# The query and key columns of four head pairs in the second layer, taken as seven half products in place of eight, with two gates between them and the values later

## The chip, the core and the metric

One core of a Trainium2 chip runs the whole kernel. The metric is the device time of one execution in microseconds (us). TensorE (PE in the profile, PEld for its weight loads) multiplies; VectorE (DVE), ScalarE (ACT) and GpSimd (POOL) do the elementwise work; the queue of SyncE (SP) issues most transfers, and GpSimd's own queue issues those that add to what lies in the destination. Each engine takes its instructions in the order in which the program has them, and waits on semaphores of the others.

## What is computed

The input x has 512 tokens of 1024 numbers, all float32. Two layers follow each other, and each is: norm, one wide input projection, a mixer over the tokens, a gate, an output projection, and a sum with x. The change touches only the second layer:

```python
def mixer_b(hn, w_in, w_out, q_gain, k_gain, rpb):      # hn = rms_norm(x, g)
    proj = hn @ w_in                                    # 512 x 1024 @ 1024 x 4096
    q, k, v, gate = jnp.split(proj, 4, axis=-1)
    q = rms_norm(q.reshape(b, s, N_HEADS, HEAD_DIM), q_gain) * (HEAD_DIM ** -0.5)
    k = rms_norm(k.reshape(b, s, N_HEADS, HEAD_DIM), k_gain)
    ...                                                 # attention on an 8 x 64 grid, 16 heads
    y = y * jax.nn.silu(gate)
    return y @ w_out
```

There are 16 heads of 64 columns. The kernel works on pairs of heads, hc = 0 to 7, of 128 columns each.

## The kernel before

**Products.** A float32 matrix is held as two rounded parts, high and low (`hn_h`, `hn_l` for the normed x; `wh`, `wl` for weights), and a product is three matmuls of 128x512 (`mm3`, line 353): high by high, high by low, low by high. One weight tile of 128x512 is loaded as half of a raw tile `wraw` (128x1024, eight of them), rounded by ScalarE (`cast`, line 173), and its low part is a subtraction `wl<-wraw,wh` on VectorE or GpSimd (`rest`, line 180). `Plan` (line 195) lists these jobs in the order of their use and says when a raw tile is loaded.

**Order of the work.** The order on TensorE is the program's order. A generator `main` walks through the projections and yields after every three matmuls or so; a generator `side` has the attention, and `run` lets it go on whenever a clock that counts the modelled matmul time has passed what `side` asked for (`later_on`, line 367, is a timer on that clock; `yield "wait", key, delay` waits for a stamp). For the other engines a scheduler decides the order at build time. What it decided can be listed from the built program.

**Second layer, main stream.** `B_MAIN` (line 43) gives the blocks in order: `("qk", n)` is queries and keys of pairs 2n and 2n+1, 512 columns (`main_qk`, line 1318), `("v", n)` values of four pairs (`main_v`), `("g", n)` the gate of one pair (`main_g`, line 1354). A block `qk` or `v` is 96 matmuls, a gate 24. `hn_h` and `hn_l` hold x times the norm's gain but not divided by the norm of the token: the division comes when results leave the accumulators, by `rs_n` (one number for each token) as ScalarE's scale, and for the gates by `rs_half`, a row of it for all partitions that `spread` makes by four transposes on TensorE (`pa<-ident,rs_n`).

**Second layer, side stream.** `side_b(hc)` (line 1379) scales a pair's queries and keys by the norms of its heads (`rawk<-rawk,rs`, VectorE, 128x1024), transposes them on TensorE (`tp<-ident,rawk`, four for the queries, four for the keys), rounds and splits them (`qh`, `ql`, `kh`, `kl`), makes scores (24 matmuls `log<-kh,qh` and the like), then exponents and their transposes. `weigh_b(hc)` multiplies with the values. `unit` (line 140) is a chain of nine small VectorE instructions (`nv`, `rs`, `na`) that makes the head norms from sums of squares (`ss<-sq`).

**First layer.** It already takes seven half products of the Strassen-Winograd form for its pairs 1 to 7 (`Plan.mixed`, line 232, and `main_a`). For that, x is first multiplied by its norm in place (`scale_x`, line 551: eight VectorE instructions `pt<-pt,pa`), split again (`renorm`, line 560), and four sums of its quarters are made and split (`mix`, line 564: `mixed<-...`, `mix_h`, `mix_l`). Weight sums are made in the raw tiles, by transfers that add (`Plan.add`, GpSimd's queue) and by VectorE (`Plan.sum`, `wraw<-wraw`).

Of the kernel before, what the change touches and what calls it, by code (L numbers as in the profile page):

```python
# [42 lines left out]
B_MAIN = [("qk", 0), ("v", 0), ("g", 0), ("qk", 1), ("g", 1), ("g", 2), ("qk", 2),  # L43
          ("g", 3), ("qk", 3), ("v", 1), ("g", 4), ("g", 5), ("g", 6), ("g", 7)]
B_COLS = {"qk": 512, "v": 512, "g": P}
# [5 lines left out]
def tile_hybrid_encoder(  # L51
# [143 lines left out]
    class Plan:  # L195
# [36 lines left out]
        def mixed(self, hc):  # L232
            b, j = hc * A_HC, len(self.jobs)
            b11, b21, b12, b22 = ([self.raw(b + 2048 * n + 1024 * i) for i in range(2)] for n in range(4))
            gate = self.raw(b - A_HC + 1152 * KT)
            v = self.raw(b - A_HC + 1024 * KT)
            t2 = [self.raw(None) for _ in range(2)]
            late = hc == 1
# [27 lines left out]
    for hc in range(1, NHC):  # L266
        plan.mixed(hc)
# [12 lines left out]
    for kind, _ in B_MAIN:  # L280
        plan.plain(at_b, B_COLS[kind], KT)
        at_b += B_COLS[kind] * KT
    outs(B_OUT)

    def lead(raw):
        return 4 if raw.first < start_jobs else 12 if raw.first < mixed_jobs else 6
# [685 lines left out]
    class turner:  # L972
# [12 lines left out]
        def send(self, dst, wait, pace, key):  # L985
# [8 lines left out]
            def read(b):  # L994
                src = d[b].rearrange("(a k) x -> k a x", a=4)
# [322 lines left out]
    def main_qk(n):  # L1318
# [24 lines left out]
    def main_v(n):  # L1343

        if not n:
            st["v"] = wk.tile([P, 4, 512], F32, tag="rawq", name="rawv", bufs=1)

        def evac(i, acc):
            act.activation(st["v"][:, i, :], acc, AF.Copy, scale=rs_n[:, i : i + 1])

        yield from project(tile_of(hn_h), tile_of(hn_l), 512, evac, ("yb", 3, "y") if n else None)
        stamp["v", n] = clock[0]

    def main_g(hc):
        acc = []
        yield from project_t(acc)
# [4 lines left out]
        src = acc[0]  # L1361
        if hc == 3:
            act.copy(gt, src)
            src = gt
        tc.keep_in_program_order(vec.tensor_mul(gt, src, st["rs_half"]))
# [131 lines left out]
    def main():  # L1497
# [7 lines left out]
        for kind, n in B_MAIN:  # L1505
            yield from {"qk": main_qk, "v": main_v, "g": main_g}[kind](n)
        yield from out_product("yb", sink_b)

    def side():
# [11 lines left out]
        for _ in scale_x():  # L1521
# [68 lines left out]
def _layout(x, norm_gain, a_w_in, a_w_out, a_q_gain, a_k_gain, t5_bias,  # L1590
# [23 lines left out]
    for kind, n in B_MAIN:  # L1614
        parts.append(cols(wb, [D * i + P * hc for i, hc in {
            "qk": [(0, 2 * n), (1, 2 * n), (0, 2 * n + 1), (1, 2 * n + 1)],
            "v": [(2, 4 * n + j) for j in range(4)],
            "g": [(3, n)],
        }[kind]]))
# [35 lines left out]
```

## Time and profile before

| | |
|---|---|
| median of 3 runs | 823.32 us (822.88 to 825.62) |
| the profiled execution | 823.05 us, of which its span (first to last instruction) is 821.3 us |
| granted TensorE clock, mean | 0.998 |
| busy share: PE, DVE, ACT, POOL | 99%, 74%, 64%, 29% |
| second layer's `spread` to the end of the span | 578.06 to 821.3 us |

The page gives busy time by engine, the chain of work that ended last, and groups of equal instructions. The trace behind it answers by stretch of time: a row of the timeline is start, length, engine, line and what was written from what, with the idle time before it and what ended that idle time in square brackets. Matmuls overlap, so the length of one is not what one costs. Most instructions of a helper share one line (L347 for matmuls, L87 for nearly all of the other engines), so rows are told apart by their tiles.

### The profile page before, as it was taken

Reading aid. Unit: us, or ns where it says so; the run is one execution under the profiler, and the core shown is the slowest. Engines: PE = TensorE matmul, PEld = TensorE weight load, DVE = VectorE, ACT = ScalarE, POOL = GpSimd, SP = SyncE. Lnnn points to the kernel's source line nnn. Section 1 sums busy time; section 2 is a strip of 40 time slices with the busy share of each in tenths; the row PEclk is TensorE's granted clock in tenths of the full one; section 3 lists DMA queues with packets and bytes.
Section 4 is the critical chain, followed back from the end, with each engine's and each line's share of the span. In section 5 each row is a group of like instructions: output and inputs, shape, how many; then the busy total and the mean of one; then the engine's idle time right before and its main releaser. Section 6 shows DMA issues by size and latency. Waiting matters only on the chain.

```text
span 821.3 us, 17411 instructions
## 1 busy us (share of the span) xinstructions
PE 812.4 (99%) x6410; PEld 659.0 (80%) x6410; DVE 610.3 (74%) x1546; ACT 522.3 (64%) x1075; POOL 235.5 (29%) x194
## 2 busy tenths in 40 slices
PE   9999999999999999999999999999999999999998
PEld 7877878788888888888888888788888887788776
DVE  7898996897887787787887886657546769776553
ACT  8668766846856856856856848554567476766340
POOL 0041402442532622622622616312111122112120
PEclk9999999999999999999999999999999999999999
DMA  9327666576585785785785664283254564634132
GB/s 348 148 65 174 169 173 161 107 213 186 125 221 165 161 212 142 162 209 146 164 206 146 143 213 157 76 314 137 102 169 144 138 198 139 197 115 139 36 103 103
DMA packets 54869, 131.92 MB, mean 161 GB/s; under 512 B 6784, under 2 KB 24384, under 8 KB 54656
## 3 DMA queue, kind: packets, MB, share of 16 engines
q1 hardware_dynamic: 48304, 108.27, 41.8%
q0 software_dynamic: 6048, 22.02, 14.7%
q8 instruction: 50, 0.82, 0.4%
q10 hardware_dynamic: 432, 0.52, 0.2%
q14 instruction: 35, 0.29, 0.1%
HBM read 111.73 MB, written 11.72 MB: 150 GB/s over the span
## 4 chain that ended last, share of the span: by engine, by line
PE 91%; DVE 4%; ACT 3%; issue 1%; DMA 0%; DVEq 0%; SPq 0%; ACTq 0%
PE acc L347 76%; PE o L347 6%; PE log L347 5%; PE tp L351 4%; DVE wl L87 1%; ACT p L87 1%; ACT wh L87 1%; DVE mixed L87 1%; ACT rawk L87 1%; DMA wraw<-in_w 0%; DVE pt L87 0%; DVE p L87 0%; DVE rawq L87 0%; PE pk L347 0%; DVE rawk L87 0%
## 5 line engine op out<-in xcount | busy, mean ns | idle before, releaser
L87 ACT CAST wh<-wraw 128x512 fp32r<-128x512 f32 (+1 forms) x344 | 206.7, 611 | 133.2 <-PE acc L347 104.9
L87 POOL TENSOR_TENSOR wl<-wraw,wh 128x512 fp32r<-128x512 f32 (+1 forms) x126 | 170.7, 1369 | 409.5 <-PE acc L347 172.5
L87 DVE TENSOR_TENSOR wl<-wraw,wh 128x512 fp32r<-128x512 f32 (+1 forms) x218 | 166.3, 766 | 60.5 <-PE acc L347 36.4
L347 PE MATMUL acc<-wh,hn_h 128*128 128x512 f32 x424 | 171.6, 406 | 0.6 <-ACT wh L87 0.3
L347 PE MATMUL acc<-wl,hn_h 128*128 128x512 f32 x424 | 165.3, 391 | 0.4 <-DVE wl L87 0.3
L347 PE MATMUL acc<-wh,hn_l 128*128 128x512 f32 x424 | 165.3, 391 | 0.0
L87 ACT ACTIVATE p<-p,mn 128x256 f32<-128x256 f32 (+2 forms) x248 | 137.9, 583 | 35.1 <-DVE mn L87 35.0
L347 PEld LDWEIGHTS acc<-wh,hn_h 128*128 128x128 f32 x424 | 79.5, 188 | 20.0 <-ACT wh L87 2.1
L347 PEld LDWEIGHTS acc<-wh,hn_l 128*128 128x128 f32 x424 | 79.6, 188 | 17.3
L347 PEld LDWEIGHTS acc<-wl,hn_h 128*128 128x128 f32 x424 | 79.8, 188 | 16.3 <-DVE wl L87 1.7
L347 PE MATMUL acc<-wh,mix_h 128*128 128x512 f32 x224 | 89.6, 400 | 0.0
L347 PE MATMUL acc<-wl,mix_h 128*128 128x512 f32 x224 | 88.1, 393 | 0.3 <-DVE wl L87 0.2
L347 PE MATMUL acc<-wh,mix_l 128*128 128x512 f32 x224 | 87.8, 392 | 0.0
L347 PE MATMUL acc<-hn_h,wh 128*128 128x512 f32 x192 | 78.4, 409 | 0.0
L347 PE MATMUL acc<-hn_h,wl 128*128 128x512 f32 x192 | 75.1, 391 | 0.0
L347 PE MATMUL acc<-hn_l,wh 128*128 128x512 f32 x192 | 75.0, 391 | 0.0
L87 DVE TENSOR_REDUCE ss<-sq 128x8 f32<-128x512 f32 (+1 forms) x80 | 44.0, 573 | 27.5 <-ACT sq L87 26.9
L87 POOL DMA_DIRECT2D wraw<-in_w x42 | 38.7, 935 | 82.4 <-DVE wl L87 35.7
L87 DVE STREAM_TRANSPOSE pt<-p 128x512 f32<-128x512 f32 (+1 forms) x60 | 40.9, 688 | 15.0 <-ACT p L87 14.2
L347 PE MATMUL acc<-y_h,wh 128*128 128x512 f32 x128 | 51.7, 404 | 0.0
L347 PEld LDWEIGHTS acc<-wh,mix_h 128*128 128x128 f32 x224 | 42.4, 189 | 10.2 <-issue 1.8
L347 PEld LDWEIGHTS acc<-wl,mix_h 128*128 128x128 f32 x224 | 42.4, 189 | 9.8 <-DVE wl L87 0.8
(152 smaller groups left out, 1330.8 us busy)
## 6 DMA issues: line engine op xcount, KB each, us to landing
wraw<-in_w SPq DMA_DIRECT2D x119, 512.0 KB
wraw<-in_w POOLq DMA_DIRECT2D x42, 512.0 KB, 7.3
pt<-pt SPq DMA_DIRECT2D x106, 64.0 KB
td<-tr SPq DMA_DIRECT2D x24, 224.0 KB
pt<-td SPq DMA_DIRECT2D x24, 224.0 KB
e<-l_d SPq DMA_DIRECT2D x32, 112.0 KB
wraw<-in_w SPq DMA_DIRECT2D x6, 384.0 KB
e<-l_d SPq DMA_DIRECT2D x16, 128.0 KB
```

The lines of the kernel that those rows point to most:

```text
L87: m = f(*args, **kw)
L347: nc.tensor.matmul(o, l, r, **kw)
L351: nc.tensor.transpose(o, i, ident)
```

## The change

Blocks 1 and 2 of the queries and keys (pairs 2 to 5) become one block `("u", 1)`. In it the 512 tokens and the 1024 rows of the product are halved, and seven products of half size in tokens and rows replace eight: 7 x 24 = 168 matmuls in place of 2 x 96 = 192. Gates 1 and 2 stand between the first products. The order of blocks becomes qk 0, gate 0, u (with gates 1 and 2), values 0, qk 3, gates 3 and 4, values 1, gates 5 to 7; before, values 0 came second.

To that end, after `spread`, x is multiplied by its norm in place (`scale_x`, now called for both layers), each slice of `hn_h` and `hn_l` is made anew as soon as gate 0 has used the old one (`renorm`, on ScalarE and in turn VectorE and GpSimd), and `mix_b` makes four sums of quarters on VectorE, their rounded parts on ScalarE and the low parts on GpSimd, into the space of `y_h` and `y_l`. Later blocks leave the accumulators by a copy, since x is already divided; gates 1 to 7 are halved by ScalarE. The weights of u are planned as those of the first layer's pairs, with four transfers that add into weights, two that add into weight sums, and two sums on VectorE. The side stream's delays change, and weighing of pairs 0 and 1 moves behind values 0.

```diff
-B_MAIN = [("qk", 0), ("v", 0), ("g", 0), ("qk", 1), ("g", 1), ("g", 2), ("qk", 2),
-          ("g", 3), ("qk", 3), ("v", 1), ("g", 4), ("g", 5), ("g", 6), ("g", 7)]
+B_MAIN = [("qk", 0), ("g", 0), ("u", 1), ("v", 0), ("qk", 3), ("g", 3), ("g", 4), ("v", 1),
+          ("g", 5), ("g", 6), ("g", 7)]
...
+        if kind == "u":
+            first_u = len(plan.jobs)
+            plan.mixed(at_b, at_b + 1024 * KT, at_b + 1152 * KT)
+            jobs_u = range(first_u, len(plan.jobs))
...
-    def project_t(acc):
+    def project_t(acc, after=None):
...
             mm3(acc[0], h, l, hn_h[:, k, :], hn_l[:, k, :], k == 0, k == KT - 1)
             yield
+            if after:
+                yield "xb", k
+                after(k)
...
-    def scale_x():
-
-        pa = spread()
+    def scale_x(pa, layer, key):
+
         for k in range(KT):
             xk = x_all[:, k, :]
-            vec.scalar_tensor_tensor(xk, xk, ng[:, 0, k : k + 1], pa, op0=ALU.mult, op1=ALU.mult)
-            stamp["xn", k] = 0
+            vec.scalar_tensor_tensor(xk, xk, ng[:, layer, k : k + 1], pa, op0=ALU.mult, op1=ALU.mult)
+            stamp[key, k] = 0
             yield 0
...
+    def mix_b():
+
+        x11, x12, x21, x22 = quarters()
+        t = wk.tile([P, 2, KH, H], F32, tag="rawq", name="mixed", bufs=1)
...
+        a, b = t[:, 0], t[:, 1]
+
+        def put(n, out, op, x, y):
+            op(out, x, y)
+            act.copy(mh[:, n], out)
+            later_on(1200, partial(split, n, out))
+
+        def split(n, out):
+            pol.tensor_sub(ml[:, n], out, mh[:, n].bitcast(F32))
+            stamp["mixb", n] = 0
+
+        for i, args in enumerate((
+            (0, a, vec.tensor_sub, x21, x22), (1, b, vec.tensor_sub, a, x11),
+            (3, b, vec.tensor_add, b, x12), (2, a, vec.tensor_sub, x11, x21),
+        )):
+            later_on(2000 + 4000 * i, partial(put, *args))
...
+    def main_u(n):
...
+        yield from product(a, hn(0, 0), True, keep)
+        yield from main_g(n)
+        yield from product(a, hn(KH, 0), False, put11)
+        yield from main_g(n + 1)
+        for m, acc, first, put in ((0, c, True, put_v), (1, b, True, put_u), (3, c, False, put12), (2, b, False, put22)):
+            yield "mixb", m
+            yield from product(acc, mixed(m), first, put, None if m else ("qk", 2 * n - 1))
+        yield from product(b, hn(KH, H), False, put21)
+        normed_b(n, r1, s1)
+        normed_b(n + 1, r2, s2)
...
     def main_g(hc):
         acc = []
-        yield from project_t(acc)
+        yield from project_t(acc, None if hc else renorm)
...
-        if hc in (1, 3, 5, 6):
-            yield "wait", ("qk", hc - 1), {1: 16000, 3: 15000, 5: 15500}.get(hc, 12000)
+        if hc in (0, 2):
+            yield "wait", ("raw", hc), 4500
         else:
-            yield "wait", ("raw", hc), 5500 if hc == 2 else 4500
+            yield "wait", ("qk", hc - 1), {1: 8000, 7: 12000}.get(hc, 9500)
...
-        act.mul(st["rs_half"], spread(), 0.5)
+        pa = spread()
+        act.mul(st["rs_half"], pa, 0.5)
         stamp["rs", "all"] = 0
+        for _ in scale_x(pa, 1, "xb"):
+            pass
+        mix_b()
         for hc in range(NHC - 2):
-            if hc >= 2:
-                yield "wait", *((("qk", hc - 1), 11000) if hc % 2 else (("raw", hc), 1500))
+            if hc == 3:
+                yield from weigh_b(0)
+                yield from weigh_b(1)
+            yield from side_b(hc)
+            if hc > 3:
                 yield from weigh_b(hc - 2)
-            yield from side_b(hc)
```

**What it moves on VectorE.** The place is the start of the second layer, from the sums of squares of qk 0 to the scaling of pair 0 that the first transposes of queries wait for. `ss` are sums of squares, `nv`, `na` and `rs` the chain of `unit`, `wl` low parts of weights, `rawk<-rawk,rs` the scaling. Before:

```order
L87 TENSOR_REDUCE ss_7118<-sq_7319 128x8
L87 TENSOR_SCALAR nv_7323<-ss_7118 128x32
L87 TENSOR_SCALAR rs_7322<-nv_7323 128x32
L87 TENSOR_TENSOR na_7324<-rs_7322 128x32
L87 TENSOR_TENSOR na_7324<-na_7324,nv_7323 128x32
L87 SCALAR_TENSOR_TENSOR na_7324<-na_7324 128x32
L87 SCALAR_TENSOR_TENSOR rs_7322<-na_7324,rs_7322 128x32
L87 TENSOR_TENSOR na_7324<-rs_7322 128x32
L87 SCALAR_TENSOR_TENSOR na_7324<-na_7324,nv_7323 128x32
L87 SCALAR_TENSOR_TENSOR rs_7322<-na_7324,rs_7322 128x32
L87 TENSOR_TENSOR wl_7376<-wraw_7180,wh_7345 128x512
L87 TENSOR_TENSOR rawk_155<-rawk_155,rs_7322 128x4x256 x2
```

The chain of nine stands in one piece, one weight split follows it, and the scaling of both pairs comes next.

Now, at the same place, first the part that ends with the second sum of quarters (`pt` is x, `hn_l` the low part made anew, `mixed` the sums of quarters):

```order
L87 SCALAR_TENSOR_TENSOR pt_97<-pt_97,pa_7303 128x512 x8
L87 TENSOR_TENSOR wl_7351<-wraw_6994,wh_7275 128x512
L87 TENSOR_REDUCE ss_7124<-sq_7322 128x8
L87 TENSOR_TENSOR hn_l_93<-pt_97,hn_h_92 128x512
L87 TENSOR_REDUCE ss_7124<-sq_7332 128x8
L87 TENSOR_TENSOR hn_l_93<-pt_97,hn_h_92 128x512
L87 TENSOR_TENSOR mixed_7317<-pt_97 128x1024
L87 TENSOR_TENSOR wl_7414<-wraw_7036,wh_7376 128x512
L87 TENSOR_TENSOR hn_l_93<-pt_97,hn_h_92 128x512 x2
L87 TENSOR_SCALAR nv_7336<-ss_7124 128x32
L87 TENSOR_TENSOR wl_7426<-wraw_7036,wh_7412 128x512
L87 TENSOR_TENSOR mixed_7317<-mixed_7317,pt_97 128x1024
```

The eight instructions of `scale_x` stand ahead of two of the sums of squares, and the chain of `unit` has only begun when two sums of quarters are done. After a further weight split, the chain's `rs`, a weight sum `wraw_7596<-wraw_6964,wraw_7219` and the chain's first `na`, the rest of the stretch is:

```order
L87 TENSOR_TENSOR mixed_7317<-pt_97 128x1024
L87 TENSOR_TENSOR na_7337<-na_7337,nv_7336 128x32
L87 SCALAR_TENSOR_TENSOR na_7337<-na_7337 128x32
L87 SCALAR_TENSOR_TENSOR rs_7335<-na_7337,rs_7335 128x32
L87 TENSOR_TENSOR mixed_7317<-mixed_7317,pt_97 128x1024
L87 TENSOR_TENSOR na_7337<-rs_7335 128x32
L87 SCALAR_TENSOR_TENSOR na_7337<-na_7337,nv_7336 128x32
L87 SCALAR_TENSOR_TENSOR rs_7335<-na_7337,rs_7335 128x32
L87 TENSOR_TENSOR rawk_155<-rawk_155,rs_7335 128x4x256
L87 TENSOR_TENSOR gt_7403<-acc_7347,rs_half_7302 128x512
L87 TENSOR_TENSOR rawk_155<-rawk_155,rs_7335 128x4x256
```

All four sums of quarters stand ahead of the scaling of pair 0, and the last of them lies in the middle of the chain. On TensorE the first transposes of queries stand where they stood: 51 matmuls behind the four transposes of `spread` (9 of qk 0, then 42 of the values before; 9 of qk 0, 24 of gate 0 and 18 of u's first product now).

**What it moves on GpSimd.** At the same place GpSimd had only weight splits, `wl<-wraw,wh`. Now it has, from the last split that belongs to the first tiles of u (`DMA` are transfers that add to weights, `y_l` the low parts of the sums of quarters):

```order
L87 TENSOR_TENSOR wl_7277<-wraw_6964,wh_7271 128x512
L87 DMA wraw_6964<-in_w 128x1024
L87 TENSOR_TENSOR wl_7378<-wraw_6994,wh_7349 128x512
L87 TENSOR_TENSOR hn_l_93<-pt_97,hn_h_92 128x512 x2
L87 DMA wraw_6994<-in_w 128x1024
L87 TENSOR_TENSOR hn_l_93<-pt_97,hn_h_92 128x512 x2
L87 TENSOR_TENSOR wl_7439<-wraw_7088,wh_7424 128x512
L87 TENSOR_TENSOR y_l_6262<-mixed_7317,y_h_6261 128x1024 x2
L87 DMA wraw_7597<-in_w 128x1024
L87 TENSOR_TENSOR y_l_6262<-mixed_7317,y_h_6261 128x1024 x2
```

Four splits of x and four of the sums of quarters have come between the weight splits. VectorE's third and fourth `mixed` write over the first and second, and so wait for the first two of these `y_l`.

More of the change, by code (lines that the diff above doesn't have):

```diff
@@ L230, in add, with mixed @@
             )
-        def mixed(self, hc):
-            b, j = hc * A_HC, len(self.jobs)
+        def mixed(self, b, gate, v, late=False):
+            j = len(self.jobs)
             b11, b21, b12, b22 = ([self.raw(b + 2048 * n + 1024 * i) for i in range(2)] for n in range(4))
-            gate = self.raw(b - A_HC + 1152 * KT)
-            v = self.raw(b - A_HC + 1024 * KT)
+            gate, v = self.raw(gate), self.raw(v)
             t2 = [self.raw(None) for _ in range(2)]
-            late = hc == 1
             order = (b11, gate, b21, b11, t2, b22, b12, v, t2) if late else (b11, gate, b21, v, b11, t2, b22, b12, t2)
@@ L266, in tile_hybrid_encoder @@
     for hc in range(1, NHC):
-        plan.mixed(hc)
+        b = hc * A_HC
+        plan.mixed(b, b - A_HC + 1152 * KT, b - A_HC + 1024 * KT, hc == 1)
     plan.plain((NHC - 1) * A_HC + 1024 * KT, 128, KT)
@@ L280, in tile_hybrid_encoder @@
     for kind, _ in B_MAIN:
-        plan.plain(at_b, B_COLS[kind], KT)
+        if kind == "u":
+            first_u = len(plan.jobs)
+            plan.mixed(at_b, at_b + 1024 * KT, at_b + 1152 * KT)
+            jobs_u = range(first_u, len(plan.jobs))
+        else:
+            plan.plain(at_b, B_COLS[kind], KT)
         at_b += B_COLS[kind] * KT
@@ L285, in lead @@
     def lead(raw):
-        return 4 if raw.first < start_jobs else 12 if raw.first < mixed_jobs else 6
+        return 4 if raw.first < start_jobs else 12 if raw.first < mixed_jobs or raw.first in jobs_u else 6
     behind, begun = [], []
@@ L562, in renorm, with quarters @@
         (pol if k % 2 else vec).tensor_sub(hn_l[:, k, :], x_all[:, k, :], hn_h[:, k, :].bitcast(F32))
+    def quarters():
+        return (x_all[:, k : k + KH, t : t + H] for t in (0, H) for k in (0, KH))
+    def mix_b():
+        x11, x12, x21, x22 = quarters()
+        t = wk.tile([P, 2, KH, H], F32, tag="rawq", name="mixed", bufs=1)
+        st["mix"] = [
+            st[y].rearrange("p (n k) (j h) -> p n (k j) h", n=4, j=2) for y in ("y_h", "y_l")
+        ]
+        mh, ml = st["mix"]
+        a, b = t[:, 0], t[:, 1]
[11 more added lines that the diff above has]
+            later_on(2000 + 4000 * i, partial(put, *args))
     def mix():
-        x11, x12, x21, x22 = (x_all[:, k : k + KH, t : t + H] for t in (0, H) for k in (0, KH))
+        x11, x12, x21, x22 = quarters()
         t = wk.tile([P, 2, KH, H], F32, tag="tr", name="mixed", bufs=1)
@@ L1322, in evac @@
         def evac(i, acc):
-            act.activation(raw[:, i, :], acc, AF.Copy, scale=rs_n[:, i : i + 1])
+            if n:
+                act.copy(raw[:, i, :], acc)
+            else:
+                act.activation(raw[:, i, :], acc, AF.Copy, scale=rs_n[:, i : i + 1])
             squares(raw[:, i, :], ss, i, 8)
@@ L1327, in main_qk, with keep, put11, put_v @@
         yield from project(tile_of(hn_h), tile_of(hn_l), 512, evac, guard)
+        normed_b(n, raw, ss)
+    def main_u(n):
+        r1, r2, s1, s2, a, b, c = part(n), part(n + 1), sums(), sums(), [], [], []
+        hn = lambda k0, t0: lambda k: (t[:, k0 + k, t0 : t0 + H] for t in (hn_h, hn_l))
+        mixed = lambda m: lambda k: (t[:, m, k, :] for t in st["mix"])
+        def keep(i, acc):
+            act.copy(r1[:, 2 + i, :], acc)
+        def put11(i, acc):
+            act.copy(r1[:, i, :], acc)
+            squares(r1[:, i, :], s1, i, 8)
+        def put_v(i, acc):
+            vec.tensor_sub(r2[:, 2 + i, :], acc, r1[:, 2 + i, :])
+        def put_u(i, acc):
+            vec.scalar_tensor_tensor(r2[:, i, :], acc, -1.0, r1[:, 2 + i, :], op0=ALU.mult, op1=ALU.subtract)
+        def put12(i, acc):
+            t = r2[:, i, :]
+            vec.tensor_add(t, t, acc)
+            squares(t, s2, i, 8)
+        def put22(i, acc):
+            t = r2[:, 2 + i, :]
+            vec.tensor_sub(t, t, acc)
+            squares(t, s2, 2 + i, 8)
+        def put21(i, acc):
+            t = r1[:, 2 + i, :]
+            vec.tensor_add(t, t, acc)
+            squares(t, s1, 2 + i, 8)
+        yield from product(a, hn(0, 0), True, keep)
[8 more added lines that the diff above has]
+        normed_b(n + 1, r2, s2)
+    def normed_b(n, raw, ss):
         rs = wk.tile([P, 32], F32, tag="rs", name="rs")
@@ L1360, in main_g @@
         eg = wk.tile([P, S], F32, tag="eg", name="eg", bufs=1)
[L1361 to L1365, printed above, removed]
+        if hc:
+            act.mul(gt, acc[0], 0.5)
+        else:
+            tc.keep_in_program_order(vec.tensor_mul(gt, acc[0], st["rs_half"]))
         act.activation(eg, gt, AF.Tanh)
@@ L1505, in main @@
         for kind, n in B_MAIN:
-            yield from {"qk": main_qk, "v": main_v, "g": main_g}[kind](n)
+            yield from {"qk": main_qk, "v": main_v, "g": main_g, "u": main_u}[kind](n)
         yield from out_product("yb", sink_b)
@@ L1520, in side @@
         stamp["rs", "a"] = 0
-        for _ in scale_x():
+        for _ in scale_x(spread(), 0, "xn"):
             pass
@@ L1614, in _layout @@
     for kind, n in B_MAIN:
[L1615 to L1619, printed above, removed]
+        for kind, n in [("qk", n), ("qk", n + 1), ("g", n), ("g", n + 1)] if kind == "u" else [(kind, n)]:
+            parts.append(cols(wb, [D * i + P * hc for i, hc in {
+                "qk": [(0, 2 * n), (1, 2 * n), (0, 2 * n + 1), (1, 2 * n + 1)],
+                "v": [(2, 4 * n + j) for j in range(4)],
+                "g": [(3, n)],
+            }[kind]]))
     parts += outs(wbo)
```

5 lines of the change are left out of this document (3 added, 2 removed).

## The prediction

> **What bounds the kernel now.** I read the page first: its span, the busy shares, and the chain of work that ended last.
>
> ```profile
> span 821.3 us, 17411 instructions
> PE 812.4 (99%) x6410; PEld 659.0 (80%) x6410; DVE 610.3 (74%) x1546; ACT 522.3 (64%) x1075; POOL 235.5 (29%) x194
> PE 91%; DVE 4%; ACT 3%; issue 1%; DMA 0%; DVEq 0%; SPq 0%; ACTq 0%
> L347 PE MATMUL acc<-wh,hn_h 128*128 128x512 f32 x424 | 171.6, 406 | 0.6 <-ACT wh L87 0.3
> ```
>
> TensorE has work 99% of the time and is 91% of the chain. A busy TensorE is not proof of a full one, so next came the waits of TensorE, longest first. Beside the 1.4 us before its first matmul the two largest are:
>
> ```profile
> PE log L347 <- ACT k L87: 1.2, 2, 0.7
> PE tp L351 <- ACT rawk L87: 1.0, 1, 1.0
> ```
>
> So it waits almost nowhere, and both ways of changing the time are plain: fewer matmuls shorten it, and any new wait of TensorE lengthens it in full. The mean of 406 ns in the group's row is not the price of a matmul, since matmuls overlap. The price comes from the chain, asked for the stretch in which the second layer starts (start, length, what, how many):
>
> ```profile
> 578.06 0.44 PE pa L351 x4
> 578.49 11.59 PE acc L347 x51
> 590.09 0.44 PE tp L351 x4
> 590.52 2.78 PE acc L347 x12
> 593.30 0.44 PE tp L351 x4
> 593.74 2.09 PE acc L347 x9
> 595.83 1.63 PE log L347 x24
> ```
>
> 51 matmuls of 128x512 in 11.59 us are 0.227 us each. The rows also give the place on which the prediction turns: the first transposes of queries (`tp`) come 11.59 us after `spread`'s (`pa`), before and after the change, because 51 matmuls lie between in both orders. What they wait for is VectorE's scaling of pair 0. The timeline of VectorE there, before:
>
> ```profile
> 578.80 0.69 DVE L87 TENSOR_REDUCE ss<-sq 128x8 f32<-128x512 f32 x1 [0.64 <-ACT sq L87]
> 583.49 0.18 DVE L87 TENSOR_SCALAR nv<-ss 128x32 f32<-128x32 f32 x1
> 583.70 0.18 DVE L87 TENSOR_SCALAR rs<-nv 128x32 int32<-128x32 int32 x1
> 586.06 1.12 DVE L87 TENSOR_TENSOR wl<-wraw,wh 128x512 fp32r<-128x512 f32 x1 [0.59 <-ACT wh L87]
> 587.10 2.35 DVE L87 TENSOR_TENSOR rawk<-rawk,rs 128x1024 f32<-128x1024 f32 x2
> ...
> 578.00:596.00 18.00, 18.00 (x89) 14.69 (x89) 10.46 (x21) 8.48 (x16) 3.89 (x3) 1.00 0.26 87
> ```
>
> The two scalings run from 587.10 to 589.45, the first done at 588.3: it is 1.8 us early. The last row is from the view by stretches (length, then busy us of PE, PEld, DVE, ACT, POOL): VectorE was busy for 10.46 of 18 us, so 7.5 us were free, part of them behind the scaling.
>
> **The change part by part.**
>
> *Fewer matmuls.* 192 become 168. 24 x 0.227 = 5.45 us less, all of it on the path. Nothing else of TensorE's main stream changes in number: gates, values and output products only trade places, and the end of the order (the last pair's scores, weights and the output product) is the same.
>
> *What VectorE gets ahead of pair 0's scaling.* By the order it has eight `pt<-pt,pa`, four `hn_l`, four `mixed`, one weight sum and two more weight splits. The first layer has all of them; here VectorE's rows, back to back:
>
> ```profile
> 28.41 5.36 DVE L87 SCALAR_TENSOR_TENSOR pt<-pt,pa 128x512 f32<-128x512 f32 x8 [1.10 <-PE pa L351]
> 33.69 0.69 DVE L87 TENSOR_TENSOR wl<-wraw,wh 128x512 fp32r<-128x512 f32 x1
> 34.29 0.68 DVE L87 TENSOR_REDUCE ss<-sq 128x8 f32<-128x512 f32 x1
> ...
> 54.58 0.68 DVE L87 TENSOR_TENSOR wl<-wraw,wh 128x512 fp32r<-128x512 f32 x1
> 55.18 0.68 DVE L87 TENSOR_TENSOR hn_l<-pt,hn_h 128x512 fp32r<-128x512 f32 x1
> ...
> 62.84 1.22 DVE L87 TENSOR_TENSOR wraw<-wraw 128x1024 f32<-128x1024 f32 x1
> 63.98 0.69 DVE L87 TENSOR_TENSOR wl<-wraw,wh 128x512 fp32r<-128x512 f32 x1
> 64.58 1.22 DVE L87 TENSOR_TENSOR mixed<-mixed,pt 128x1024 f32<-128x1024 f32 x1
> ```
>
> From start to start: eight `pt` 5.28 us, a 512-wide instruction 0.60, a 1024-wide one 1.14; a small one of the chain takes 0.21 (583.49 to 583.70). So 5.28 + 4 x 0.60 + 5 x 1.14 + 2 x 0.60 = 14.6 us are added. Were all the 7.5 free us ahead of the scaling, and with the 1.8 by which it was early, 14.6 - 7.5 - 1.8 = 5.3 us would still be left. VectorE cannot be in time.
>
> *How late, at least.* Follow the order as if every engine ran undisturbed. The second sum of squares starts at 578.80, so the `pt` start at 579.4 and end at 584.7. Then five 512-wide instructions (587.7), the first `mixed` (588.8), three 512-wide, `nv` and one split (591.5), the second `mixed` (592.6). The fourth `mixed` writes over the second, whose rounded part (ScalarE) and low part (GpSimd) must be taken first. Their rows from the first layer:
>
> ```profile
> 65.83 1.05 ACT L87 CAST mix_h<-mixed 128x1024 fp32r<-128x1024 f32 x1 [0.33 <-DVE mixed L87]
> 47.05 1.38 POOL L87 TENSOR_TENSOR hn_l<-pt,hn_h 128x512 fp32r<-128x512 f32 x1 [1.78 <-ACT hn_h L87]
> 50.68 2.90 POOL L87 TENSOR_TENSOR mix_l<-mixed,mix_h 128x1024 fp32r<-128x1024 f32 x1 [2.25 <-PE acc L347]
> 51.24 3.41 DVE L87 TENSOR_TENSOR mixed<-mixed,pt 128x1024 f32<-128x1024 f32 x1
> 585.33 1.29 POOL L87 TENSOR_TENSOR wl<-wraw,wh 128x512 fp32r<-128x512 f32 x1 [4.15 <-PE acc L347]
> ```
>
> 592.6 + 1.05 + 2.90 + 1.22 = 597.8, three small ones of the chain 598.4, the scaling 1.18 (half of 2.35): 599.6. TensorE, due at 590.1, would wait 9.5 us.
>
> *How late, if the two engines exclude each other.* The row at 51.24 says that they do: VectorE's sum, 1.22 us alone, took 3.41, and it ended at 54.65, 1.07 us after GpSimd's `mix_l` (50.68 + 2.90 = 53.58). The split at 586.06 shows the same: 1.12 in place of 0.69, beside GpSimd's from 585.33. Instructions of VectorE that read only one operand, or one from an accumulator, show no such stretch (the `pt` and `ss` above are of that kind). So from 584.7 on, lengths add. GpSimd, which has just finished a split then (its buffer comes free with the first half of gate 0, 578.5 + 21 x 0.227 = 583.3, plus 1.29), must do four `hn_l`, one split and two `y_l` before the fourth `mixed`: 4 x 1.38 + 1.29 + 2 x 2.90 = 12.6 us. VectorE does four splits and four `hn_l` (4.8), five 1024-wide (5.7), nine small ones (1.9) and the scaling (1.18): 13.6 us; its two `ss` may run beside GpSimd. 584.7 + 12.6 + 13.6 = 610.9, a wait of 20.8 us. I take this end, since the rows show the exclusion each time that both want two operands from memory; 9.5 remains the lower bound.
>
> A part of this wait comes earlier, at the first product's third matmul, which needs the first new `hn_l`; it is the same delay, not a second one. Behind the waiting transposes stand all matmuls: TensorE's queue has nothing else to do.
>
> The Trainium skill (SBUF — State Buffer, section "SBUF: two separate sides") says that the port pair these two engines share belongs to whichever instruction starts first, for its whole length, and that the other blocks. Read as turns, one instruction each, that rule gives the sum of this text, 840.0; this trace has a case in which GpSimd went twice in a row (the rows at 79.36 and 79.99 below), and by that the time would be 845.8.
>
> *The clock.* After waits the trace shows a slower TensorE. The two waits of the scores in the first layer (the 1.2 us above, around 78 us) were followed by this (by stretches, the third column from the end is the granted clock; then TensorE's rows):
>
> ```profile
> 79.00:82.00 3.00, 3.00 (x72) 2.29 (x73) 2.48 (x2) 1.48 (x2) 3.00 (x4) 0.70 0.74 115
> 82.00:85.00 3.00, 3.00 (x12) 2.35 (x11) 2.96 (x8) 0.62 (x1) 2.04 (x3) 0.73 1.00 190
> ...
> 81.44 0.63 PE L347 MATMUL acc<-wl,mix_h 128*128 128x512 f32 x1
> 81.86 0.63 PE L347 MATMUL acc<-wh,mix_l 128*128 128x512 f32 x1
> ```
>
> Matmuls 0.42 apart, and (0.30 + 0.27) x 3 / 0.5 = 3.4 us at half clock. That is eight matmuls at 0.2 us more: 1.6 us, once, after the long wait.
>
> *What costs nothing.* Twelve more weight tiles are rounded and split in u, its ten combining instructions run on VectorE, and gates are halved on ScalarE. In the 52 us from 596 on, VectorE and ScalarE are free for about a third:
>
> ```profile
> 596.00:622.00 26.00, 26.00 (x138) 21.37 (x138) 13.71 (x44) 15.56 (x41) 3.89 (x3) 1.00 0.54 167
> 622.00:648.00 26.00, 26.00 (x150) 21.20 (x149) 20.38 (x55) 18.13 (x45) 6.51 (x5) 1.00 0.60 168
> ```
>
> Free on VectorE: 12.3 + 5.6 = 17.9 us. Added: twelve splits at most (7.2), ten combinations (6.0), one sum (1.1): 14.3. It fits, with little to spare; if it doesn't, the third rival is the price. The transfers that add are issued by GpSimd and are due several tiles later, as in the first layer; among the waits of TensorE none is put down to a transfer.
>
> *The sum*, against the profiled execution's own 823.05 us (its span and 1.75 us around; the median of the runs, 823.32, is 0.03% above): 823.05 - 5.45 + 20.8 + 1.6 = 840.0 us.
>
> **The rivals.**
>
> *The engines share after all.* Then the wait is 9.5 us: 823.05 - 5.45 + 9.5 + 1.6 = 828.7, and anything up to about 835 if some instructions slip past each other. For it: a few 1024-wide scalings kept their 1.2 us beside GpSimd. Against it: the 3.41 us. Chance 0.22.
>
> *Faster.* The scaling's lateness stays inside what the 24 matmuls save: 823.05 - 5.45 = 817.6 at best. It decides at a scaling done by 590.1 + 5.4 = 595.5, 4.1 us before my lower bound. For it: 7.5 us of VectorE were free. Against it: even with every free moment used, the 5.3 us left above eat up the 5.45 saved. Chance 0.07. That the seven products are not there is no rival: the order has 24 rows fewer on TensorE.
>
> *More waits behind the first.* GpSimd can hold the place twice in a row:
>
> ```profile
> 79.36 3.19 POOL L87 TENSOR_TENSOR wl<-wraw,wh 128x512 fp32r<-128x512 f32 x2
> 79.99 3.65 DVE L87 TENSOR_TENSOR mix_l<-mixed,mix_h 128x1024 fp32r<-128x1024 f32 x1 [0.52 <-ACT mix_h L87]
> ```
>
> If the last two `y_l` go ahead of the chain, 2 x 2.90 = 5.8 us come on top: 845.8; and if they hold VectorE between the scaling and `kl`, the scores wait some 2 us more: 848. Chance 0.15.
>
> **How the numbers follow.** The forecast (835 to 845) has 0.56. The range, 827 to 848, leaves out the faster case (0.07) and about 0.05 at either end of the other two. About 0.3% (2.5 us) is what a measurement of this kernel can tell from no change. Faster by more: 0.06; within: 0.04, from the edges of the first two rivals; slower: 0.90.
>
> **What would show it.** Right: among TensorE's waits a new one, `tp` for VectorE's `rawk`, of some 18 to 21 us, with one of about 2 us for `hn_l` before it; eight `pt` of 5.3 us after `pa`; `mixed` and `hn_l` of VectorE at 2 to 4 us beside GpSimd's `y_l`; a half clock for 3.4 us behind. Wrong: transposes less than 6 us after their old place, or VectorE's instructions keeping 0.69 and 1.22 us beside GpSimd's. A wait in the u block's later products, or for an adding transfer, would make the place wrong even if the time were right.

## The result, and the profile after

The changed kernel takes 847.87 us (median of 4 runs, 845.04 to 848.37), the kernel before 823.48 us on the same chip. The ratio is 1.0282, with a 95% interval of 1.0257 to 1.0307: slower by 24 us. The forecast was 840.0 us, in a range of 827 to 848, and slower with a chance of 0.90. The profiled execution took 848.37 us, of which its span is 846.6.

First the head of the page after:

```profile
span 846.6 us, 17500 instructions
PE 813.4 (96%) x6386; PEld 658.2 (78%) x6386; DVE 637.8 (75%) x1574; ACT 536.6 (63%) x1101; POOL 263.4 (31%) x213
```

TensorE has 24 matmuls less (6386 for 6410) and almost the same busy time, but a span 25.3 us longer: it waits now. Its waits, longest first (us in total, times, longest):

```profile
PE tp L355 <- DVE rawk L87: 21.7, 1, 21.7
PE acc L351 <- DVE rawk L87: 1.6, 2, 1.0
...
PE acc L351 <- DVE hn_l L87: 0.7, 1, 0.7
```

One row is nearly the whole result: the first transposes of the second layer's queries wait 21.7 us for VectorE's scaling of pair 0. The other two are new as well, and small: `hn_l` in the first product of u, and the accumulators of u's last product (`acc` for `rawk`).

The chain of waits around that place (start, length, what), to be held against the rows of before at 590.09 to 595.83:

```profile
611.30 2.27 DVE na L87
...
613.83 1.24 DVE rawk L87
...
615.11 1.11 PE tp L355 x4
616.22 5.08 PE acc L351 x12
621.31 0.43 PE tp L355 x4
621.74 2.09 PE acc L351 x9
...
663.08 0.41 DVE wl L87
663.48 0.60 DVE rawk L87
664.08 1.09 DVE wl L87
```

The twelve matmuls behind the transposes take 5.08 us in place of 2.78; and at 663 a second, small stop shows, where VectorE takes weight splits between the sums that empty u's accumulators.

What VectorE did until 613.83, from its timeline:

```profile
581.77 5.35 DVE L87 SCALAR_TENSOR_TENSOR pt<-pt,pa 128x512 f32<-128x512 f32 x8
...
591.05 5.21 DVE L87 TENSOR_TENSOR mixed<-pt 128x1024 f32<-128x1024 f32 x1
...
597.99 2.32 DVE L87 TENSOR_SCALAR nv<-ss 128x32 f32<-128x32 f32 x1
600.22 0.68 DVE L87 TENSOR_TENSOR wl<-wraw,wh 128x512 fp32r<-128x512 f32 x1
...
603.87 2.33 DVE L87 TENSOR_TENSOR na<-rs 128x32 f32<-128x32 f32 x1
...
608.93 2.34 DVE L87 TENSOR_TENSOR na<-rs 128x32 f32<-128x32 f32 x1
611.30 2.26 DVE L87 SCALAR_TENSOR_TENSOR na<-na,nv 128x32 f32<-128x32 f32 x1
```

And GpSimd's timeline over the same time:

```profile
591.13 2.82 POOL L87 TENSOR_TENSOR hn_l<-pt,hn_h 128x512 fp32r<-128x512 f32 x2
593.64 1.52 POOL L87 TENSOR_TENSOR wl<-wraw,wh 128x512 fp32r<-128x512 f32 x1
597.41 2.85 POOL L87 TENSOR_TENSOR y_l<-mixed,y_h 128x1024 fp32r<-128x1024 f32 x1 [2.25 <-ACT y_h L87]
603.19 2.96 POOL L87 TENSOR_TENSOR y_l<-mixed,y_h 128x1024 fp32r<-128x1024 f32 x1 [2.92 <-ACT y_h L87]
...
608.50 5.02 POOL L87 TENSOR_TENSOR y_l<-mixed,y_h 128x1024 fp32r<-128x1024 f32 x2 [1.53 <-ACT y_h L87]
```

Read the two together, by their ends. VectorE's first `mixed` starts at 591.05 and ends at 596.26, 1.1 us (its own length) after GpSimd's split ends at 595.16: it stood for three of GpSimd's instructions. Four instructions of the chain on 128x32 numbers, 0.18 us otherwise, take 2.26 to 2.34, each beside one `y_l`; one of the four, `nv<-ss`, reads a single tile. Where GpSimd is still (600.22), VectorE's 0.68 is the length of an undisturbed split. VectorE counts as busy for all of this time, but 4.0 us of the `mixed` and 2.1 of each of the four small ones, 12.4 of the 23 us from 591 on, are standing.

The clock, by stretches (third column from the end):

```profile
596.00:602.00 6.00, 0.00 (x0) 0.00 (x0) 6.00 (x8) 2.08 (x3) 2.85 (x1) 0.60 0.03 4
...
614.00:620.00 6.00, 4.89 (x14) 4.02 (x15) 4.12 (x7) 2.91 (x6) 1.28 (x1) 0.50 0.00 0
620.00:626.00 6.00, 6.00 (x44) 4.71 (x43) 2.58 (x9) 2.07 (x5) 0.00 (x0) 0.91 0.16 48
```

It falls during the wait and comes back at 621.1 (the last stretch: 0.91 is 4.9 of 6 us at full), 6 us after TensorE went on.

**Where 25.3 us come from**, by the distances between TensorE's matmuls, after against before:

| | us |
|---|---|
| 24 fewer matmuls | -5.45 |
| wait for the first `hn_l` | +0.8 |
| wait for pair 0's scaling | +21.8 |
| half clock behind it | +2.8 |
| two waits for accumulators in u's last product | +2.0 |
| pair 2's scores and small gaps | +1.0 |
| first product of the first layer | +2.3 |

The last row is not the change's: both kernels do the same there, and the profiled execution after was 2.2 us late by the first transposes of the first layer. Run again (a0_again, below), the kernel was only 0.3 us late when the second layer began, and its long wait was the same 21.7 us. There the half clock cost 2.4 us in place of 2.8.

### The profile page after: what moved, and what is told of

Its sections match the earlier page's. It is cut to its first block, busy times and chain, and to the rows that moved or that the text cites. A ratio compares the mean times of both kernels' runs of the same rounds, so it can differ in the third digit from the quotient of the medians.

```text
span 846.6 us, 17500 instructions
## 1 busy us (share of the span) xinstructions
PE 813.4 (96%) x6386; PEld 658.2 (78%) x6386; DVE 637.8 (75%) x1574; ACT 536.6 (63%) x1101; POOL 263.4 (31%) x213
## 5 line engine op out<-in xcount | busy, mean ns | idle before, releaser
L87 ACT CAST wh<-wraw 128x512 fp32r<-128x512 f32 (+1 forms) x356 | 214.0, 611 | 134.0 <-PE acc L351 113.0
L87 POOL TENSOR_TENSOR wl<-wraw,wh 128x512 fp32r<-128x512 f32 (+1 forms) x131 | 177.4, 1368 | 360.0 <-PE acc L351 171.9
L351 PE MATMUL acc<-wh,hn_h 128*128 128x512 f32 x384 | 157.4, 411 | 2.5 <-DVE rawk L87 1.6
L351 PE MATMUL acc<-wl,hn_h 128*128 128x512 f32 x384 | 151.0, 395 | 0.4 <-DVE wl L87 0.3
L351 PE MATMUL acc<-wh,hn_l 128*128 128x512 f32 x384 | 150.7, 394 | 0.7 <-DVE hn_l L87 0.7
L351 PEld LDWEIGHTS acc<-wh,hn_h 128*128 128x128 f32 x384 | 72.8, 190 | 21.2 <-ACT wh L87 3.7
L351 PEld LDWEIGHTS acc<-wh,hn_l 128*128 128x128 f32 x384 | 72.8, 190 | 17.2 <-DVE hn_l L87 1.1
L351 PEld LDWEIGHTS acc<-wl,hn_h 128*128 128x128 f32 x384 | 73.1, 190 | 14.8 <-DVE wl L87 1.5
L87 POOL DMA_DIRECT2D wraw<-in_w x48 | 43.9, 928 | 95.3 <-DVE wl L87 36.8
L351 PE MATMUL acc<-y_h,wl 128*128 128x512 f32 x128 | 50.0, 391 | 0.0
```

The lines of the kernel that those rows point to most:

```text
L87: m = f(*args, **kw)
L351: nc.tensor.matmul(o, l, r, **kw)
```

## The experiments

All are edits of the changed kernel. The theory: VectorE and GpSimd keep each other out whenever both want two operands from memory, so their work ahead of pair 0's scaling adds up. The first rival: the delay comes from VectorE's queue alone, or from its waiting for buffers that GpSimd has yet to read.

### e1_vec: no low part on GpSimd

```diff
-            pol.tensor_sub(ml[:, n], out, mh[:, n].bitcast(F32))
+            vec.tensor_sub(ml[:, n], out, mh[:, n].bitcast(F32))
```

The eight `hn_l` of gate 0 go to VectorE as well.

> All low parts of the new work (the eight hn_l made anew and the four y_l) go to VectorE, none to GpSimd: VectorE gets 4 x 0.60 + 4 x 1.14 = 7.0 us more of its own, GpSimd loses 4 x 1.38 + 4 x 2.90 = 17.1 us. Theory (the two engines exclude each other): the wait of the first transposes falls from 21.7 us to 14 to 17 us, VectorE's small instructions are back at 0.2 us and mixed at 1.2, and the time is about 841. Rival (VectorE's own queue is simply too long and GpSimd runs beside it): the wait grows by the 7 us less what mixed no longer waits for, to 24 to 28 us, and the time is 850 or more.

840.07 us (839.16 to 840.63); 1.0207 of before, 1.0192 to 1.0222. From its waits and VectorE's timeline:

```profile
PE tp L355 <- DVE rawk L87: 17.2, 1, 17.2
```

```profile
604.64 0.18 DVE L87 SCALAR_TENSOR_TENSOR na<-na 128x32 f32<-128x32 f32 x1
604.74 1.21 DVE L87 TENSOR_TENSOR y_l<-mixed,y_h 128x1024 fp32r<-128x1024 f32 x1
```

and one row of GpSimd's:

```profile
589.45 5.72 POOL L87 TENSOR_TENSOR wl<-wraw,wh 128x512 fp32r<-128x512 f32 x1 [2.32 <-ACT wh L87]
```

VectorE got 7 us more to do, and the wait is 4.5 us shorter. The small instructions are back at 0.18, and `y_l` costs VectorE 1.21 where it had cost GpSimd 2.9 and VectorE the standing. The wait is 0.2 us above the expected band, the direction and the time are the theory's. That VectorE's queue alone is at fault is excluded. It has a large part all the same: of the 17.2 us that are left, 7.0 are the work moved there, so that some 10 us of the long wait (an estimate from these two numbers) belong to VectorE's own queue and the other half to its standing beside GpSimd.

### e5_own: a buffer of their own for the last two sums

```diff
+        t2 = wk.tile([P, 2, KH, H], F32, tag="tr", name="mixed2", bufs=1)
-            (3, b, vec.tensor_add, b, x12), (2, a, vec.tensor_sub, x11, x21),
+            (3, t2[:, 0], vec.tensor_add, b, x12), (2, t2[:, 1], vec.tensor_sub, x11, x21),
```

> The third and fourth sum of quarters get a buffer of their own, so that VectorE never waits for ScalarE's or GpSimd's taking of the first two; y_l stays on GpSimd. Theory (exclusion): nothing changes in the amount of work that excludes each other, the wait of the first transposes stays at 18 to 22 us, time 844 to 848. Rival (VectorE waits for the buffer, a dependency and not a lock): the wait falls to 7 to 11 us, time 833 to 837.

844.98 us (844.87 to 845.56); 1.0269, 1.0254 to 1.0284.

```profile
PE tp L355 <- DVE rawk L87: 15.2, 1, 15.2
PE acc L351 <- DVE hn_l L87: 5.2, 2, 2.9
```

The long wait alone would fit neither. But the first sum now stands ahead of VectorE's `hn_l`, and part of the same delay is paid there, at u's first product: 15.2 + 5.2 = 20.4 us, inside the theory's 18 to 22. The buffers explain at most the 2.0 us between this and the changed kernel's 21.7 + 0.7.

### e2_order: the scaling ahead of the sums

The chain, the scaling of pairs 0 and 1, and each sum are held to the program's order; the sums are put 12 us later (14000 + 4500 for each in place of 2000 + 4000). `y_l` stays on GpSimd.

> The four sums of quarters and their splits come behind pair 0's scaling in VectorE's order; y_l stays on GpSimd. Ahead of the scaling are left, behind the eight pt: four hn_l, four splits, one weight sum, the chain and the scaling, 8.5 us, and on GpSimd four hn_l and a split, 6.8 us. Theory (exclusion): the wait of the first transposes falls to 5 to 9 us, since lengths still add but y_l is out; time about 830 to 834. Rival (no exclusion, the order alone): 2 to 3 us and a time of 824 to 827. If the sums are then missed by the third of the seven products, a wait for y_l or y_h shows there instead.

840.41 us (839.83 to 840.83); 1.0211, 1.0193 to 1.0228.

```profile
PE tp L355 <- DVE rawk L87: 9.5, 2, 8.7
PE log L351 <- DVE kl L87: 3.2, 1, 3.2
```

The wait at the place is as expected, 8.7 us, and one row of VectorE's timeline shows the exclusion without any sum:

```profile
589.00 4.68 DVE L87 TENSOR_TENSOR wl<-wraw,wh 128x512 fp32r<-128x512 f32 x1
```

A split of 0.68 us stood for GpSimd's two `hn_l` and a split. But the time missed the expectation by 6 us and more. 13 us were taken from the long wait and about 7 arrived: the sums, now behind, made pair 1's scaling (0.8 us of the first row) and its `kl` late, and a second half clock followed. The edit has a hand in this: it holds pair 1's scaling behind the sums too, 19.7 us behind pair 0's (598.77 and 618.52), where it came 1.7 us behind in the changed kernel (613.83 and 615.57). That opened the next question: is it only the place, or is VectorE full?

### e3_tp: the transposes 6 us later

```diff
-            yield "wait", ("raw", hc), 4500
+            yield "wait", ("raw", hc), 10500 if hc == 0 else 4500
```

> The transposes of pair 0 are put 6 us later into TensorE's order; VectorE's and GpSimd's orders change only by three combinations of gate 0 (about 1.3 us) that now come ahead of the scaling. Theory (TensorE waits for a scaling that is done at a fixed time): the wait shrinks by 6 less 1.3 us, to 16 to 18 us, and the time by about 5. Rival (the work ahead of the scaling is itself held up by TensorE, so it moves along): the wait stays at 20 to 22 us and the time at 847.

843.77 us (843.47 to 847.67); 1.0264, 1.0241 to 1.0287.

```profile
PE tp L355 <- DVE rawk L87: 12.5, 1, 12.5
PE acc L351 <- DVE wl L87: 3.3, 4, 1.7
```

The matmuls that came ahead of the transposes now wait for their own weight splits, some 3 us, so up to the scaling it is 12.5 + 3 in all, just under the expected 16 to 18; and behind it a `kl` is 2.1 us late. 9 us less at the place, 3 to 4 less in time, against about 5 expected.

### g8_eight: the preparation alone

Eight products in before's order, with gate 0 ahead of values 0; x is scaled in place and split again, no sums. TensorE's order around pair 0 is that of before.

```diff
+B_MAIN = [("qk", 0), ("g", 0), ("v", 0), ("qk", 1), ("g", 1), ("g", 2), ("qk", 2),
+          ("g", 3), ("qk", 3), ("v", 1), ("g", 4), ("g", 5), ("g", 6), ("g", 7)]
...
-        mix_b()
```

> Eight products as before, in before's order but with gate 0 ahead of values 0; x is still scaled in place and split again during gate 0, the four sums and their splits are left out. TensorE's order is the same as before's around pair 0, so what is added is the preparation alone. Ahead of the scaling VectorE has eight pt (5.3 us) and four hn_l (2.4), GpSimd four hn_l and a split (6.8). Theory (exclusion): the first transposes wait 6 to 8 us, with the clock behind it the time is 832 to 835. Rival (GpSimd's part is free, and the sums and y_l make nearly all of the delay): 1 to 3 us, 824 to 827.

831.42 us (830.52 to 833.89); 1.0099, 1.0073 to 1.0124.

```profile
PE tp L356 <- DVE rawk L87: 4.9, 1, 4.9
```

VectorE's `hn_l` and a split:

```profile
586.27 1.18 DVE L87 TENSOR_TENSOR hn_l<-pt,hn_h 128x512 fp32r<-128x512 f32 x1
...
587.97 1.18 DVE L87 TENSOR_TENSOR hn_l<-pt,hn_h 128x512 fp32r<-128x512 f32 x1
589.07 1.78 DVE L87 TENSOR_TENSOR wl<-wraw,wh 128x512 fp32r<-128x512 f32 x1
590.77 2.37 DVE L87 TENSOR_TENSOR hn_l<-pt,hn_h 128x512 fp32r<-128x512 f32 x2
```

beside GpSimd's four:

```profile
585.15 6.84 POOL L87 TENSOR_TENSOR hn_l<-pt,hn_h 128x512 fp32r<-128x512 f32 x4
```

4.9 us is between the two expectations (6 to 8, and 1 to 3), and the time is just below the first one's band. Adding all lengths was too much: here the two engines took turns, and five splits of VectorE, 3.0 us alone, became 1.10 + 1.10 + 1.70 + 2.30 = 6.2 us from start to start. With 0.8 for the first `hn_l` and 2.4 at half clock the preparation costs 8.3 us, and behind it TensorE's matmuls stay 8.3 us late to the end. So the preparation alone costs more than the 5.45 us that the 24 matmuls can bring.

### f4_vec_tp15, h2_order_vec, h1_order_vec: the place, or a full VectorE?

All three have the low parts on VectorE. f4_vec_tp15 puts pair 0's transposes 48 matmuls later (delay 15000). h2_order_vec puts them 30 later (11000), holds the chain and the scaling of pairs 0 and 1 to the program's order, and has one sum ahead of pair 0's; h1_order_vec 48 later, with two sums ahead.

> All low parts on VectorE as in e1_vec, and pair 0's transposes 48 matmuls (10.9 us) later in TensorE's order. Theory A (only the place of the wait counts; VectorE has room later): the wait of the transposes falls from 17.2 to 7 to 9 us and the time from 840 to 829 to 831. Theory B (VectorE is full until the u block ends: in e1_vec it is busy for 35.2 of the 40 us from 615 to 655, so 4.8 us are free): most of what is won at the transposes comes back as waits of the scores, or of the u block for VectorE's sums or accumulators; the time stays at 834 to 838.

> All low parts on VectorE, the transposes of pair 0 30 matmuls (6.8 us) later, and only the first of the four sums (with its y_l) ahead of the scaling. Ahead of the scaling VectorE has 7 us less than in e1_vec and some 2 us of splits more: done at 602 to 604, due at 597.8. Theory A (place alone): a wait of 4 to 6 us, 1 to 2 us at kl, time 827 to 830. Theory B (VectorE full): the three sums that go behind, 7 us, come back in the u block: time 832 to 836.

> As h2_order_vec, but the transposes 48 matmuls (10.9 us) later, and two sums ahead of the scaling. Scaling done at 605 to 607, due at 601.8. Theory A: a wait of 3 to 5 us, time 826 to 829. Theory B: 831 to 835, with waits at the scores of pairs 0 and 1, which now follow each other closely, and in the u block's later products.

843.00 us (842.79 to 844.93), 840.06 (839.44 to 842.53) and 842.31 (840.89 to 842.86); ratios 1.0239 (1.0222 to 1.0257), 1.0204 (1.0183 to 1.0225) and 1.0223 (1.0206 to 1.0240). Not one is measurably below e1_vec's 840.07, and all three are above even theory B's bands. TensorE's waits of f4_vec_tp15:

```profile
PE tp L355 <- DVE rawk L87: 13.0, 1, 13.0
PE log L351 <- DVE kl L87: 2.6, 1, 2.6
```

and of h2_order_vec:

```profile
PE tp L355 <- DVE rawk L87: 12.3, 2, 6.3
```

In f4_vec_tp15 the transposes came 10.9 us later and the wait fell by 4.2, because the weight splits for the 48 matmuls ahead came in front of the scaling; the rest came back at pair 1's scores, `kl` and (1.6 us) ScalarE's `kh`, with a second half clock. In h2_order_vec pair 0 waits 6.2 us (expected 4 to 6), and then pair 1's scaling, behind the sums, makes a second wait of as much; h1_order_vec waits 9.0 and 5.6 us at these two places. Here too the edit has a hand in the second wait, since it holds pair 1's scaling back. The two scalings of h2_order_vec:

```profile
602.26 1.23 DVE L87 TENSOR_TENSOR rawk<-rawk,rs 128x1024 f32<-128x1024 f32 x1
...
629.57 1.18 DVE L87 TENSOR_TENSOR rawk<-rawk,rs 128x1024 f32<-128x1024 f32 x1
```

In f4_vec_tp15, which does not hold it, pair 1's scaling followed pair 0's at once, and the second waits (1.6 and 2.6 us) were shorter. Theory A is excluded as it was put, since what was won at the place did not arrive; theory B has the direction, but not the size. The stretch from the scaling of x to the end of u, by engine: before, then f4_vec_tp15, then h2_order_vec:

```profile
580.00:655.00 75.00, 75.00 (x407) 61.19 (x406) 48.00 (x132) 42.82 (x104) 14.18 (x11) 1.00 0.48 144
```

```profile
580.00:655.00 75.00, 57.73 (x273) 46.71 (x272) 66.00 (x139) 48.62 (x110) 27.07 (x18) 0.86 0.48 115
```

```profile
580.00:655.00 75.00, 60.33 (x284) 48.24 (x282) 67.37 (x145) 50.96 (x115) 27.46 (x19) 0.91 0.58 135
```

TensorE goes from 75 busy us to 58 or 60, VectorE from 48 to 66 or 67 (65.8 in e1_vec). At 655 us e1_vec and h2_order_vec are at u's last product, and f4_vec_tp15 is some 3 us short of it. Up to there VectorE is busy 8.3 us longer than TensorE in f4_vec_tp15 and 7.0 in h2_order_vec, more than the 24 matmuls bring. But VectorE is not full over the whole stretch: of the 75 us it was idle for 9.0 and 7.6. So about half of TensorE's 17.3 and 14.7 idle us comes from the amount of VectorE's work, and half from times in which VectorE itself stood idle. How much a better order would win is open; one with values 0 ahead of u, as the kernel before has them ahead of its later queries, was not tried.

### c1_less: less work behind the scaling

h2_order_vec with three of the four `y_l` left out, all of them behind pair 0's scaling.

> As h2_order_vec, with three of the four y_l left out (the u block's second to fourth product of sums then read what lay in that space): 3 x 1.14 = 3.4 us less of VectorE's work, all of it behind pair 0's scaling, the order otherwise the same. Theory (VectorE is the bound from the spread to the end of the u block, so each us of its work there costs about one): the waits at kl and at pair 1's scaling shrink, and the time falls by 3 to 5 us, from 840.1 to 835 to 837. Rival (only pair 0's scaling is late, later work is covered by matmuls): at most 1 us less.

834.31 us (833.70 to 836.02); 1.0134, 1.0116 to 1.0152: 5.7 us less than h2_order_vec (5.0 between the profiled spans), a little below the expected band.

```profile
PE tp L355 <- DVE rawk L87: 9.8, 2, 6.0
```

The first wait is the same (6.2 us, start to start), the second falls from 6.4 to 4.0, and the waits for `kh` and `kl` ahead of pair 0's scores (0.4 and 1.0 us) are gone. In h2_order_vec one of these `y_l` had cost 2.96 us beside a split of GpSimd, so the three were 5.4 us of VectorE's time, and 5.0 to 5.7 us went. In this order, work behind the place is not covered by matmuls. That each us of VectorE's work up to the end of u counts is not shown by it: all three stood ahead of pair 1's scaling, which this order holds back.

### d1_busy: the clock alone

92 matmuls into the bank of the transposes, ahead of them, which nobody reads:

```diff
+        for _ in range(fill):
+            nc.tensor.matmul(tp, hn_h[:, 0, :P], hn_h[:, 1, :], start=True, stop=True)
```

> The changed kernel itself once more, on the same chip as the next two, for their comparison: 847 to 848 us, and 845 to 846 where its start is not 2.2 us late.

> 92 matmuls that nobody reads (20.9 us at 0.227) ahead of pair 0's first transposes, in the same accumulator bank: TensorE works through its wait instead of standing still, and only the clock can differ. Theory (a half clock follows the wait and costs 2.8 us): the clock stays at full, matmuls behind the transposes are 0.227 apart at once, and the time is 2 to 3 us below the changed kernel's. Rival (the matmuls at 0.43 us behind the wait are held back by something else, weights or accumulators): no difference.

a0_again 847.07 us (844.80 to 848.11); d1_busy 844.19 us (843.99 to 845.74), with ratios 1.0282 (1.0263 to 1.0301) and 1.0255 (1.0238 to 1.0271). The two intervals overlap; the trace decides. Behind the transposes of d1_busy, in the timeline of TensorE:

```profile
615.05 0.39 PE L351 MATMUL acc<-wh,hn_h 128*128 128x512 f32 x1
615.28 0.39 PE L351 MATMUL acc<-wl,hn_h 128*128 128x512 f32 x1
```

0.23 apart at once, where the changed kernel's are these:

```profile
617.30 0.63 PE L351 MATMUL acc<-wh,hn_h 128*128 128x512 f32 x1
617.73 0.63 PE L351 MATMUL acc<-wl,hn_h 128*128 128x512 f32 x1
```

The 0.43 us matmuls were the clock and nothing else. Between the first and the second four transposes lie 6.03 us in the changed kernel and 3.23 here (3.21 before): 2.8 us.

### d2_puts: the small waits at u's last product

The sums that empty the accumulators (`put12`, `put22`, `put21`) are held to the program's order on VectorE.

> The sums that empty the accumulators of the u block's last three products are held to the program's order on VectorE, so that one split less stands between two of them. Theory (the 1.96 us of waits for accumulators there come from splits that VectorE does in between): the second wait (0.8 us over a matmul) goes, the first stays, since three splits still stand ahead of the first sum; 0.5 to 1 us less. Rival (VectorE is late there as a whole): no difference, or the split that now comes later is missed instead.

848.57 us (848.22 to 848.81); 1.0303, 1.0289 to 1.0318.

```profile
PE acc L351 <- DVE rawk L87: 3.2, 2, 2.2
```

The theory failed: the waits grew from 1.6 to 3.2 us, since a weight split (one of them 1.76 us beside GpSimd's) and a reduction of ScalarE's squares now stand between each of the last three sums; the clock went to half once more, from 663.2 to 666.6. It is not the order of two splits: VectorE is late there, and in the changed kernel it is busy for 6.00 of the 6 us from 656 to 662.

## Why the prediction was right, and where it was off

1. *24 fewer matmuls, -5.45.* 24 instructions are gone, and a matmul still takes 0.227. Taken from the count and the distance; not tried by itself.
2. *VectorE's scaling is the wait that takes the place.* Right, in place and in cause: `tp` for `rawk`, and no other long one. *The engines exclude each other, 20.8 us.* Right as the choice between the ends: e1_vec gave VectorE more work and a shorter wait, e5_own took the buffers away and left 20.4 us. With the 0.8 us before it the delay is 22.6. That 20.8 lies so near is in part luck, since two errors of opposite sign stand behind it: two more `y_l`, 5.0 us, stood ahead of the scaling than the sum had (the third rival's condition), and some 3 us of the other lengths did not add up, because `hn_l` on both engines partly overlapped (g8_eight). The part at the first `hn_l` was 0.8, not 2 us. One reading was wrong as well: VectorE's instructions with a single operand were taken as exempt, by rows of `pt` and `ss` beside which GpSimd was still. A sum `ss` beside GpSimd does keep its 0.68 us (before, 35.49), but `nv<-ss`, 0.18 us alone, took 1.29 beside an `hn_l` in the kernel before (40.91) and 2.32 beside a `y_l` after. The sum is not touched by it, since it added the chain in full.
3. *Half clock, 1.6 us.* The mechanism was right, the size not: 2.8 us (d1_busy; 2.4 in a0_again). The row it was priced by, 3.4 us after two waits of under a microsecond, was not the price of the row at hand: the clock came back 6 us after TensorE went on (4.9 in a0_again, after the same wait).
4. *What costs nothing.* This step failed. The 14.3 us of splits and sums were set against 17.9 free us of before between 596 and 648, an average over 52 us. Where that work is due there is no such room: VectorE is busy for 6.00 of the 6 us from 656 to 662, u's last product then waits 2.0 us, d2_puts could not order it away, and what was saved at the transposes came back in large part (e2_order, f4_vec_tp15, h2_order_vec; in the first and the last partly by their own hold on pair 1). The prediction had named a wait in u's later products as a sign that the place was wrong; it came, but as 2 of 25 us.
5. *The sum.* -5.45 + 21.8 + 0.8 + 2.8 + 2.0 + 0.5 for pair 2's scores = 22.5 us, against 17.0 forecast (a0_again's span is 844.0, 22.7 above before's 821.3, 0.3 of it from the start). Of the 5.5 us that are missing, 1.8 are the wait, 1.2 the clock, 2.5 the step that "costs nothing". The rest to the median, some 2 us, is what the profiled execution lost in the first product of the first layer; whether the other executions lost it there too is not shown. The median, 847.87, lies 0.1 us inside the end of the range and 7.9 us from the forecast, so it is the place and the cause of the wait that speak for the prediction, more than the number.

The rivals: that the engines share (828.7) is excluded by e1_vec. A scaling that kept its length beside GpSimd, as this rival had it, was simply first: in the kernel before, beside the two at 720.77, it was GpSimd's split that grew (722.70, 1.57 us for 1.29). Faster was out of reach by more than the prediction said: even without any sum the preparation costs 8.3 us in the order of g8_eight. The third rival's time, 845.8 to 848, was met, and so was its condition, all four `y_l` ahead of the scaling; but of its price only the first part came, and the 2 us for scores behind `kl` did not.

The Trainium skill (SBUF — State Buffer, section "SBUF: two separate sides") says that the pair of ports belongs to whichever starts first for the whole of its instruction. The trace agrees, and in both directions: a 128x32 instruction stood 2.1 us for a `y_l`, and in e1_vec a split of GpSimd, 1.3 us alone, took 5.72 beside a packed VectorE. Who asked first can't always be read from the rows: the first `mixed` begins at 591.05, GpSimd's `hn_l` at 591.13, and yet `mixed` stood, but its row also overlaps the one before it by 0.07 us. Nothing here shows turns as a rule: three of GpSimd's instructions went past that one waiting `mixed`.

No version tried beats the kernel before. The cheapest ones that compute everything with seven products, e1_vec and h2_order_vec, are 17 us above it.

## What to carry to other kernels

Before saving matmuls, add up the elementwise work that the saving needs over the stretch in which it must be done, and compare it with the matmul time of that stretch: here VectorE was busy for 7 us more than TensorE, against 5.45 to be won, before any question of order. Free time is to be counted in the stretch where the work is due, not as an average behind it. And a helper engine that shares its way to memory with the engine that is late makes it later: moving the low parts from GpSimd to VectorE, more work for the late engine, was 7 us faster.

## What the runs showed of the hardware that was not expected

- How small a VectorE instruction is doesn't protect it: 128x32 numbers, 0.18 us alone, took 2.26 to 2.34 us beside a 128x1024 subtraction of GpSimd, four times in one chain; nor does a single operand (`nv<-ss`, 2.32).
- GpSimd can go past a waiting VectorE instruction three times (the first `mixed`, 5.21 us for 1.21; in e2_order a split, 4.68 for 0.68).
- The way back to the full clock took 3.3 us after one wait (e1_vec, 17.2 us of wait) and 6 us after another (21.8), but 4.9 when the same program waited as long again (a0_again); a wait of 2.9 us was enough for a half clock (e5_own: half from 589.3 to 592.7, behind a stop at 585.6).
- Two profiled executions of one program differed by 2.1 us before anything of the second layer ran. 1.5 us of it were there by the first layer's first transposes and arose in the first 12 us, where one had begun 26 matmuls and the other 33 (36 in the kernel before).
